# Gate operands' low parts by token halves, a first set of sigmoids one slot earlier, and one weight copy moved behind a partial sum's copy

## The chip, the cores and the metric

The kernel runs on one core of a Trainium2 chip. The metric is the device time of one execution in microseconds (us); for several runs the median is given. A core has a matrix engine (PE, with PEld for its weight loads), a vector engine (DVE), an engine for activations and copies (ACT), a third elementwise engine (POOL) and a queue that issues transfers (SP). Each engine takes its instructions strictly in the order in which the program lists them, and each waits on semaphores for the others.

## The reference

One hybrid decoder layer on 2048 tokens of 1024 channels, all in float32:

```python
xn = rms_norm(h, ln_g)
proj = jnp.einsum('bsd,de->bse', xn, w_in)          # 1024 -> 6 groups of 1024 columns
b_gate, c_gate, x_conv, g_conv, x_lru, g_lru = jnp.split(proj, splits, axis=-1)
y_conv = b_gate * causal_conv3(c_gate * x_conv);  y_conv = headnorm(y_conv) * silu(g_conv)
u = causal_conv4(x_lru) + bias
r = sigmoid(blockdiag(w_a) u + b_a);  i = sigmoid(blockdiag(w_i) u + b_i)
a = exp(8 r log_sigmoid(lam));  hidden_t = a_t hidden_{t-1} + sqrt(1 - a_t^2) i_t u_t
y_lru = headnorm(hidden) * silu(g_lru)
out = rms_norm(h + concat(y_conv, y_lru) @ w_out)
```

The two gates r and i of the recurrence come from small block-diagonal products of u. "Gate" below means these.

## The kernel before

**Products.** Channels stand on the 128 partitions, tokens along the free axis. The work is a list of 64 steps. For each half h of the sequence (1024 tokens) and each block k of 128 channels there are three steps: `l` (the columns x_lru and g_lru), `a` (c_gate and x_conv) and `b` (b_gate and g_conv); then come 16 steps `o` of the output projection. The steps of h = 0 run from about 97 to 510 us, those of h = 1 to about 1000 us. A step is a 2 x 2 block product by a Strassen-like scheme: seven products (numbered 0 to 6) of a weight operand S and an activation operand T, summed in the PSUM banks A, B and C. To keep float32 precision each operand is held as a high part, which is a rounding cast, and a low part, which is the value less the high part; a product is 12 matmuls (four inner blocks, high x high, high x low, low x high).

**Order within a step.** All instructions stand in an order written by hand; a "slot" is one product of PE. A usual step has the slots 0 to 6 with the products 0, (6 of the step before), 1, 3, 2, 4, 5. Bank A takes products 0, 1, 2 and 5, one upon the other, and three partial sums of it are copied away by ACT between them: `q1` after product 0, `u2` after product 1, `rr` after product 2 (line L1305, "the third partial sum's copy"; the tiles of u2 and rr change names every step). Product 1 can't start before q1 has been copied, product 2 not before u2, product 5 not before rr; between a sum's end and its next use lies one other product.

**Weights of the next step.** While step n runs, `s_plan` makes the seven S operands of step n+1, one piece in each slot: `add(i)` forms a sum on DVE, `hi(i)` casts a high part on ACT (L200), `lo(i)` makes a low part on DVE, or on POOL for operands 0, 4 and 6. In slot 4, beside product 2, stand `hi(3)` and `lo(1)`. The value cast by hi(3) is a difference that `add(3)` made on DVE two slots before (`raw<-raw` in the profile).

**Later work.** `at(n, f)` puts f into the n-th slot from now; `tick()` runs what is due at the start of a slot. The recurrence of block k begins when its x_lru is complete, at the end of step `l`. Its own slots count from there: 1 to 7 lie in step `a`, 8 to 14 in step `b`. `sth` (slot 5) casts the high parts of u for the gates on ACT, `stl` (slot 6) makes the low parts on DVE; two tiles `st` hold them, in st[0] the high part of channels 0 to 63 above their low part, in st[1] the low part of channels 64 to 127 above their high part. `gates(0)` in slot 8 runs four gate matmuls (st[0] twice, st[1] twice) over the first 512 tokens, `gates(1)` in slot 10 the same over the other 512; both use the same two PSUM buffers, so that `gates(1)` waits for the sigmoids that read the first. `sigs(i)` are these four sigmoids on ACT (L743, 64 x 512 each). For h = 0 `sigs(0)` stood in slot 9 and for h = 1 in slot 8; `sigs(1)` in slots 11 and 10.

Of the kernel before, what the change touches and what calls it, by code (L numbers as in the profile page):

```python
# [12 lines left out]
F32 = mybir.dt.float32  # L13
F32R = mybir.dt.float32r
AF = mybir.ActivationFunctionType
ALU = mybir.AluOpType
# [4 lines left out]
C = 512  # L21
# [17 lines left out]
def hymba_kernel(ctx: ExitStack, tc: tile.TileContext, x, xt, w_in, par, lamc, w_gate, w_out, final_g, out):  # L39
# [122 lines left out]
    def tt(out, a, b, op, eng=None):  # L162
        (eng or nc.vector).tensor_tensor(out=out, in0=a, in1=b, op=op)  # L163
# [6 lines left out]
    def low(v, hl, eng=None):  # L170
        tt(hl[1], v, hl[0].bitcast(F32), ALU.subtract, eng)

    def s_tile(dst, i):
        t = sp.tile([P, 2, C], F32R, tag="s", name="s")
        dst[i] = (t[:, 0, :], t[:, 1, :])
        return t


    def s_plan(n, r, dst):
        a11, a12, a21, a22 = r  # L180
        t, tiles = {}, {}

        def add(i):
            if i == 2:
                t[2] = aux("s1")
                tt(t[2], a21, a22, ALU.add)
            elif i == 1:
                t[1] = aux("s2")
                tt(t[1], t[2], a11, ALU.subtract)
            elif i == 3:  # L190
                tt(a21, a11, a21, ALU.subtract)
            else:
                tt(t[1], a12, t[1], ALU.subtract)

        def val(i):
            return {0: a11, 1: t.get(1), 2: t.get(2), 3: a21, 4: a12, 5: t.get(1), 6: a22}[i]

        def hi(i):
            tiles[i] = s_tile(dst, i)
            nc.scalar.copy(dst[i][0], val(i))  # L200

        def lo(i, eng=None):
            low(val(i), dst[i], eng)
            if PLAIN <= n < 3 * KT:
                at(3 if eng else 2, lambda: nc.sync.dma_start(sd[n][i], tiles[i].bitcast(F32)))

        g = nc.gpsimd if PLAIN < n < 3 * KT else None
        return [lambda: (add(2), add(1)),
                lambda: (hi(0), lo(0, g), add(3)),
                lambda: hi(1),  # L210
                lambda: (hi(3), lo(1)),
                lambda: (hi(2), lo(3), add(5)),
                lambda: (hi(4), lo(4, g), lo(2)),
                lambda: hi(5),
                lambda: (hi(6), lo(6, g), lo(5))]
# [21 lines left out]
    class TPrep:  # L237
# [8 lines left out]
        def hi(self, i, v=None):  # L246
            self.dst[i, self.j] = hl = t_tile(i, self.j)
            nc.scalar.copy(hl[0], self.val(i) if v is None else v)
# [445 lines left out]
    def lru(h, k, late=0, early=0):  # L694
        o1 = wt("o1", "xl", n=N2 + 4)
        g = wt("o2", "gl", bufs=O2)
        if h == 0:
            nc.gpsimd.memset(o1[:, 0:4], 0.0)
        else:
            nc.scalar.copy(o1[:, 0:4], hx[:, k, :])  # L700
        v = {}
        lw = [pt[:, LW + 8 * j + k:LW + 8 * j + k + 1] for j in range(4)]

        def c0():
            v["u"] = wt("u", "u")
            nc.scalar.activation(out=v["u"], in_=o1[:, 1:1 + N2], func=AF.Identity, scale=lw[0],  # L706
                                 bias=pt[:, LB + k:LB + k + 1])

        def cj(j):
            nc.vector.scalar_tensor_tensor(out=v["u"], in0=o1[:, 1 + j:1 + j + N2], scalar=lw[j],  # L710
                                           in1=v["u"], op0=ALU.mult, op1=ALU.add)

        def keep():
            if h == 0:
                nc.scalar.copy(hx[:, k, :], o1[:, N2:N2 + 4])

        def sth():
            v["st"] = st = hl_tile("st", 2)
            at(6, lambda: hl_done(2))
            for j, hi in enumerate((LO, HI)):  # L720
                nc.scalar.copy(st[j][hi], v["u"][hi])

        def stl():
            st = v["st"]
            for j, (hi, lo) in enumerate(((LO, HI), (HI, LO))):
                tt(st[j][lo], v["u"][hi], st[j][hi].bitcast(F32), ALU.subtract)

        def gates(i):
            sl = slice(i * C, (i + 1) * C)
            if i == 0:  # L730
                v["r"], v["i"] = wt("r", "r"), wt("ig", "i", bufs=IG)
            v["ps"] = ps = []
            for j in range(2):
                ps.append(pss.tile([P, C], F32, tag="s", name="gate"))
                for n in range(2):
                    nc.tensor.matmul(ps[j], v["gw"][n][:, j, :], v["st"][j][:, sl],  # L736
                                     start=(n == 0), stop=(n == 1))

        def sigs(i):
            sl = slice(i * C, (i + 1) * C)  # L740
            for j, (hi, lo) in enumerate(((LO, HI), (HI, LO))):
                for g_, src, bias in ((v["r"], hi, BA), (v["i"], lo, BI)):
                    nc.scalar.activation(out=g_[hi, sl], in_=v["ps"][j][src], func=AF.Sigmoid,  # L743
                                         bias=pt[src, bias + k:bias + k + 1])


        def s0():
            tt(v["u"], v["i"], v["u"], ALU.mult)

        def s1():  # L750
            v["T"] = wt("ig", "T", bufs=IG)
            nc.scalar.activation(out=v["T"], in_=v["r"], func=AF.Tanh, scale=nklam[:, k:k + 1])

        def s1b():
            nc.scalar.activation(out=v["r"], in_=v["r"], func=AF.Exp, scale=klam[:, k:k + 1])

        def s2():
            nc.scalar.activation(out=v["T"], in_=v["T"], func=AF.Sqrt)

        def s3():  # L760
            nc.vector.scalar_tensor_tensor(out=v["u"], in0=v["r"], scalar=1.0, in1=v["u"],
                                           op0=ALU.add, op1=ALU.mult)

        def s4():
            tt(v["u"], v["T"], v["u"], ALU.mult)

        def s5():
            r = v["r"]
            init = 0.0 if h == 0 else hl[:, k:k + 1]
            nc.vector.tensor_tensor_scan(out=r, data0=r, data1=v["u"], initial=init,  # L770
                                         op0=ALU.mult, op1=ALU.add)
            if h == 0:
                nc.vector.tensor_copy(hl[:, k:k + 1], r[:, N2 - 1:N2])

        def out_():
            finish(0, h, KT + k, v["r"], g, pt[:, LG + k:LG + k + 1])

        def gw():
            v["gw"] = load_gate_w(k)

        def put(which, bank, other):
            dst = {11: o1[:, 4:4 + C], 12: o1[:, 4 + C:4 + N2], 21: g[:, 0:C], 22: g[:, C:N2]}[which]
            combine(dst, bank, other)
            if which == 12:
                at(1, c0)
                at(2, lambda: cj(1), lambda: cj(2), keep, gw)
                at(3, lambda: cj(3))
                for slots, *fs in ((5 - early, sth), (6 - early, stl), (8, lambda: gates(0)), (9 - h - early, lambda: sigs(0)),
                                   (10, lambda: gates(1)), (11 - h - early, lambda: sigs(1)), (12, s1, s0),
                                   (13, s1b), (14, s2, s3), (15, s4), (16, s5), (17, out_)):  # L790
                    at(slots + late, *fs)
            if which == 21:
                silu(g, late, nc.vector if h and late else None)

        return put
# [236 lines left out]
    def prep(n, s):  # L1032
        if n < N:
            plan[n][s]()
# [3 lines left out]
    with tc.manual_schedule(engines={ENG.PE, ENG.Activation, ENG.DVE, ENG.Pool, ENG.SP}):  # L1038
# [177 lines left out]
        for n in range(PLAIN, N):  # L1216
            kind, h, k = steps[n]
# [28 lines left out]
            for s in range(6 if late else 8 if new or last else 7):  # L1246
# [24 lines left out]
                if new and s > 0:  # L1271
                    if s in (1, 3, 4, 5):
                        prep(n + 1, (1, 3, 4, 5).index(s) + 1)
                    elif s > 5:
                        prep(n + 2, s - 5)
                elif s > 0:
                    prep(n + 1, s - 1)
                if s == 3:
                    load_next(n + 2, 3 if late else 4)
# [17 lines left out]
                if i == 0:  # L1297
                    q1 = sm_q1[0] = sm("q1")
                    nc.scalar.copy(q1, bk["A"])  # L1299
                elif i == 1:  # L1300
                    u2 = sm_u2[0] = sm(("u2", "rr")[n % 2])
                    nc.scalar.copy(u2, bk["A"])  # L1302
                elif i == 2:
                    rr = sm(("rr", "u2")[n % 2])
                    nc.scalar.copy(rr, bk["A"])  # L1305
                    put(22, bk["B"], rr)
                    if late:
                        put(12, bk["D"], rr)
                elif i == 4:
                    put(11, bk["C"], q1)  # L1310
                elif i == 5 and not late:
                    put(12, bk["A"], None)
                elif i == 6:
                    put(21, bk["B"], u2)
# [50 lines left out]
```

## Time and profile before

| what | value |
|---|---|
| median of 3 runs | 1325.04 us (1324.93 to 1326.69) |
| the profiled execution | 1325.2 us, its span 1323.4 us |
| granted clock of the matrix engine | 0.997 |
| matmul busy | 1293.5 us of the span (98%) |
| DVE, ACT, POOL busy | 1040.3, 749.1, 245.2 us |

The profile gives for every instruction its start and duration, and for an idle time before it the event that ended it. Matmuls overlap, so a lost time on PE is read from the starts: undisturbed ones follow each other every 0.23 us.

### The profile page before, as it was taken

Reading aid. Unit: us, or ns where it says so; the run is one execution under the profiler, and the core shown is the slowest. Engines: PE = TensorE matmul, PEld = TensorE weight load, DVE = VectorE, ACT = ScalarE, POOL = GpSimd, SP = SyncE. Lnnn points to the kernel's source line nnn. Section 1 sums busy time; section 2 is a strip of 40 time slices with the busy share of each in tenths; the row PEclk is TensorE's granted clock in tenths of the full one; section 3 lists DMA queues with packets and bytes.
Section 4 is the critical chain, followed back from the end, with each engine's and each line's share of the span. In section 5 each row is a group of like instructions: output and inputs, shape, how many; then the busy total and the mean of one; then the engine's idle time right before and its main releaser. Section 6 shows DMA issues by size and latency. Waiting matters only on the chain.

```text
span 1323.4 us, 16676 instructions
## 1 busy us (share of the span) xinstructions
PE 1293.5 (98%) x5688; PEld 1058.0 (80%) x5688; DVE 1040.3 (79%) x1252; ACT 749.1 (57%) x1141; POOL 245.2 (19%) x189
## 2 busy tenths in 40 slices
PE   7989999999999999999999999999999999999997
PEld 6868878787878787878888888888888788887886
DVE  7789898999989897978566676667549777649886
ACT  7576758566675657466554545364457433445453
POOL 3204233344334340002010110101011000000000
PEclk9999999999999999999999999999999999999999
DMA  7138787888989888542789999999779887697654
GB/s 292 32 116 292 279 288 251 299 327 277 339 289 324 294 295 300 195 157 74 247 314 297 333 354 332 338 350 363 237 273 330 267 257 239 235 404 276 231 181 160
DMA packets 157958, 355.29 MB, mean 268 GB/s; under 512 B 16944, under 2 KB 51760, under 8 KB 157872
## 3 DMA queue, kind: packets, MB, share of 16 engines
q1 hardware_dynamic: 153264, 338.17, 73.7%
q0 software_dynamic: 4320, 15.73, 3.1%
q8 instruction: 45, 0.74, 0.2%
q14 instruction: 41, 0.34, 0.1%
q10 hardware_dynamic: 288, 0.32, 0.1%
HBM read 217.11 MB, written 137.04 MB: 268 GB/s over the span
## 4 chain that ended last, share of the span: by engine, by line
PE 55%; DVE 22%; DMA 10%; issue 6%; ACT 6%; SPq 1%; POOL 0%; DVEq 0%; ACTq 0%; POOLq 0%
PE bank L999 53%; DVE s L163 5%; DVE tl L163 2%; DVE u L710 2%; DMA s<-so 2%; PE gate L736 2%; DMA sd<-s 1%; DVE st L163 1%; DVE r L770 1%; DMA raw<-in_w_in_dram 1%; DMA xr<-od 1%; DVE sums L641 1%; DVE traw L163 1%; ACT i L743 1%; ACT r L743 1%
## 5 line engine op out<-in xcount | busy, mean ns | idle before, releaser
L999 PE MATMUL bank<-th,s 128*128 128x512 f32 x3632 | 1130.2, 390 | 9.6 <-ACT rr L1302 2.8
L999 PEld LDWEIGHTS bank<-th,s 128*128 128x128 f32 x3632 | 682.1, 188 | 157.4 <-ACT rr L1302 4.1
L999 PE MATMUL bank<-tl,s 128*128 128x512 f32 x1816 | 707.8, 390 | 1.8 <-DVE tl L163 1.6
L999 PEld LDWEIGHTS bank<-tl,s 128*128 128x128 f32 x1816 | 341.1, 188 | 75.0 <-DVE tl L163 3.4
L163 POOL TENSOR_TENSOR s<-raw,s 128x512 fp32r<-128x512 f32 x62 | 110.6, 1796 | 245.8 <-ACT s L200 207.4
L200 ACT CAST s<-raw 128x512 fp32r<-128x512 f32 x140 | 85.3, 618 | 76.4 <-PE bank L999 45.4
L163 POOL TENSOR_TENSOR gb<-gb,sg 128x1024 f32<-128x1024 f32 x16 | 43.4, 2712 | 336.4 <-ACT sg L669 298.2
L163 DVE TENSOR_TENSOR s<-raw,s 128x512 fp32r<-128x512 f32 (+1 forms) x125 | 93.1, 768 | 10.6 <-ACT s L1058 6.7
L163 DVE TENSOR_TENSOR s<-s,s 128x512 fp32r<-128x512 f32 x105 | 85.5, 814 | 1.9 <-ACT s L200 1.4
L163 DVE TENSOR_TENSOR tl<-traw,th 128x512 fp32r<-128x512 f32 x85 | 60.8, 748 | 23.1 <-ACT th L438 16.9
L200 ACT CAST s<-s 128x512 fp32r<-128x512 f32 x105 | 64.9, 618 | 12.6 <-DVE s L163 12.5
L710 DVE SCALAR_TENSOR_TENSOR u<-xl,pt,u 128x1024 f32<-128x1024 f32 x48 | 61.5, 1280 | 7.8 <-ACT u L706 7.2
L1299 ACT COPY q<-bank 128x512 f32<-128x512 f32 x58 | 34.0, 585 | 54.0 <-PE bank L999 44.4
L820 DVE SCALAR_TENSOR_TENSOR t<-p,pt,t 128x1024 f32<-128x1024 f32 x32 | 46.5, 1454 | 16.6 <-ACT t L817 15.9
L743 ACT ACTIVATE r<-gate,pt 64x512 f32<-64x512 f32 x64 | 43.8, 684 | 17.4 <-PE gate L736 16.6
L1302 ACT COPY rr<-bank 128x512 f32<-128x512 f32 x31 | 18.1, 584 | 55.2 <-PE bank L999 55.2
L163 DVE TENSOR_TENSOR st<-u,st 64x1024 fp32r<-64x1024 f32 x32 | 47.2, 1476 | 1.0
L1302 ACT COPY u<-bank 128x512 f32<-128x512 f32 x27 | 15.8, 585 | 53.4 <-PE bank L999 53.4
L163 DVE TENSOR_TENSOR raw<-raw 128x512 f32<-128x512 f32 x41 | 44.9, 1095 | 0.2
L438 ACT CAST th<-traw 128x512 fp32r<-128x512 f32 x64 | 36.2, 618 | 15.6 <-DVE traw L163 13.9
L743 ACT ACTIVATE i<-gate,pt 64x512 f32<-64x512 f32 x64 | 43.8, 685 | 1.1
L163 DVE TENSOR_TENSOR traw<-traw 128x512 f32<-128x512 f32 x60 | 42.3, 709 | 2.2 <-DMA traw<-in_w_out_dram 1.1
(169 smaller groups left out, 1267.4 us busy)
## 6 DMA issues: line engine op xcount, KB each, us to landing
sd<-s SPq DMA_DIRECT2D x151, 512.0 KB
s<-sd SPq DMA_DIRECT2D x151, 512.0 KB
raw<-in_w_in_dram SPq DMA_DIRECT2D x104, 256.0 KB
raw<-yd SPq DMA_DIRECT2D x64, 256.0 KB
traw<-in_w_out_dram SPq DMA_DIRECT2D x64, 256.0 KB
so<-so SPq DMA_DIRECT2D x22, 512.0 KB
s<-so SPq DMA_DIRECT2D x22, 512.0 KB
yd<-gl SPq DMA_DIRECT2D x32, 256.0 KB
```

Source lines behind the costliest of these rows:

```text
L163: (eng or nc.vector).tensor_tensor(out=out, in0=a, in1=b, op=op)
L200: nc.scalar.copy(dst[i][0], val(i))
L438: nc.scalar.copy(self.dst[i, j][0], self.r[i, j])
L641: nc.vector.tensor_reduce(out=sums[0][:, kt * R:(kt + 1) * R].rearrange("p (q b) -> p q b", q=4), in_=y.rearrange("p (b q a) -> p q b a", ...
L710: nc.vector.scalar_tensor_tensor(out=v["u"], in0=o1[:, 1 + j:1 + j + N2], scalar=lw[j], in1=v["u"], op0=ALU.mult, op1=ALU.add)
L736: nc.tensor.matmul(ps[j], v["gw"][n][:, j, :], v["st"][j][:, sl], start=(n == 0), stop=(n == 1))
L743: nc.scalar.activation(out=g_[hi, sl], in_=v["ps"][j][src], func=AF.Sigmoid, bias=pt[src, bias + k:bias + k + 1])
L770: nc.vector.tensor_tensor_scan(out=r, data0=r, data1=v["u"], initial=init, op0=ALU.mult, op1=ALU.add)
L820: nc.vector.scalar_tensor_tensor(out=tcur["t"], in0=p[:, 2 + j:2 + j + N2], scalar=cw[j], in1=tcur["t"], op0=ALU.mult, op1=ALU.add)
L999: nc.tensor.matmul(bank, a[:, js], b, start=start and n == 0, stop=stop and n == 2, skip_group_check=more)
L1299: nc.scalar.copy(q1, bk["A"])
L1302: nc.scalar.copy(u2, bk["A"])
```

## The change

It has three parts.

1. `stl` makes the low parts in four pieces of 64 x 512 instead of two of 64 x 1024, first both tiles' first token half, then both tiles' second half. This holds for all 16 recurrences.
2. `sigs(0)` is always due in slot 8, in the same slot as `gates(0)`. That moves it for the blocks 1 to 7 of h = 0; for the others it was there already.
3. In slots whose product is number 2, hi(3) of the next step's weights is held back and issued right behind the copy `rr`. In the whole program 32 of the 58 copies change places with it.

```diff
+    held = [None]
+    def defer(f):
+        if held[0] is None:
+            f()
+        else:
+            held[0].append(f)
+    def release():
+        fs, held[0] = held[0] or (), None
+        for f in fs:
+            f()
...
-                lambda: (hi(3), lo(1)),
+                lambda: (defer(lambda: hi(3)), lo(1)),
...
         def stl():
             st = v["st"]
-            for j, (hi, lo) in enumerate(((LO, HI), (HI, LO))):
-                tt(st[j][lo], v["u"][hi], st[j][hi].bitcast(F32), ALU.subtract)
+            for i in range(2):
+                sl = slice(i * C, (i + 1) * C)
+                for j, (hi, lo) in enumerate(((LO, HI), (HI, LO))):
+                    tt(st[j][lo, sl], v["u"][hi, sl], st[j][hi, sl].bitcast(F32), ALU.subtract)
...
-    (8, lambda: gates(0)), (9 - h - early, lambda: sigs(0)),
+    (8, lambda: gates(0)), (8, lambda: sigs(0)),
...
                 elif s > 0:
+                    held[0] = [] if i == 2 else None
                     prep(n + 1, s - 1)
...
                     nc.scalar.copy(rr, bk["A"])
+                    release()
                     put(22, bk["B"], rr)
```

No instruction is added or removed on PE, ACT, POOL or SP, and on PE, POOL and SP the order is the same; DVE has 32 instructions more. Line numbers of the changed kernel are 13 to 16 higher.

On ACT, in step `l` of block 4 of h = 0 (slots 3 to 5), before: a sigmoid of the step before, a weight cast, a square, then hi(3) as the cast of a `raw` tile, and the copy `rr` behind it.

```order
L669 ACTIVATE sg_2667<-gb_2406 128x1024
L200 CAST s_2669<-s2_2627 128x512
L661 ACTIVATE r_2410<-r_2410 128x1024
L200 CAST s_2697<-raw_2506 128x512
L1305 COPY rr_2712<-bank_2603 128x512
L200 CAST s_2719<-s1_2625 128x512
```

The same place now:

```order
L682 ACTIVATE sg_2675<-gb_2414 128x1024
L213 CAST s_2677<-s2_2635 128x512
L674 ACTIVATE r_2418<-r_2418 128x1024
L1321 COPY rr_2718<-bank_2611 128x512
L213 CAST s_2720<-raw_2514 128x512
L213 CAST s_2727<-s1_2633 128x512
```

The copy and the cast have changed places; what is behind them stands as before.

On ACT, where step `a` of block 4 ends and its step `b` begins (the gates of block 4), before: the copy of p out of bank A, hi(5) as the cast of an `s2` tile, the copy q1, and the four sigmoids of the first token half.

```order
L200 CAST s_2907<-raw_2673 128x512
L799 COPY p_2756<-bank_2763 128x512
L200 CAST s_2938<-s2_2788 128x512
L1299 COPY q1_2953<-bank_2940 128x512
L743 ACTIVATE r_2928<-gate_2930,pt_164 64x512
L743 ACTIVATE i_2929<-gate_2930,pt_164 64x512
L743 ACTIVATE r_2928<-gate_2933,pt_164 64x512
L743 ACTIVATE i_2929<-gate_2933,pt_164 64x512
L817 ACTIVATE t_2989<-p_2756,pt_164 128x1024
```

The same place now:

```order
L213 CAST s_2917<-raw_2681 128x512
L814 COPY p_2764<-bank_2771 128x512
L758 ACTIVATE r_2938<-gate_2940,pt_164 64x512
L758 ACTIVATE i_2939<-gate_2940,pt_164 64x512
L758 ACTIVATE r_2938<-gate_2943,pt_164 64x512
L758 ACTIVATE i_2939<-gate_2943,pt_164 64x512
L213 CAST s_2952<-s2_2796 128x512
L1315 COPY q1_2967<-bank_2954 128x512
L832 ACTIVATE t_2999<-p_2764,pt_164 128x1024
```

The four sigmoids have moved ahead of hi(5) and q1.

On DVE, ahead of the gates of block 4, before: the sum xx, the two low parts `st`, then low parts and sums for the next step's weights.

```order
L163 TENSOR_TENSOR xx_2881<-bank_2844,u2_2879 128x512
L163 TENSOR_TENSOR st_2857<-u_2759,st_2857 64x1024
L163 TENSOR_TENSOR st_2858<-u_2759,st_2858 64x1024
L163 TENSOR_TENSOR s_2864<-raw_2672,s_2864 128x512
L163 TENSOR_TENSOR s2_2788<-raw_2673,s2_2788 128x512
```

The same place now:

```order
L163 TENSOR_TENSOR xx_2889<-bank_2852,u2_2885 128x512
L163 TENSOR_TENSOR st_2865<-u_2767,st_2865 64x512
L163 TENSOR_TENSOR st_2866<-u_2767,st_2866 64x512
L163 TENSOR_TENSOR st_2865<-u_2767,st_2865 64x512
L163 TENSOR_TENSOR st_2866<-u_2767,st_2866 64x512
L163 TENSOR_TENSOR s_2887<-raw_2680,s_2887 128x512
L163 TENSOR_TENSOR s2_2796<-raw_2681,s2_2796 128x512
```

Two instructions have become four, and a gate matmul over the first 512 tokens waits for the first two of them alone.

More of the change, by code (lines that the diff above doesn't have):

```diff
@@ L787, in put @@
                 at(3, lambda: cj(3))
-                for slots, *fs in ((5 - early, sth), (6 - early, stl), (8, lambda: gates(0)), (9 - h - early, lambda: sigs(0)),
+                for slots, *fs in ((5 - early, sth), (6 - early, stl), (8, lambda: gates(0)), (8, lambda: sigs(0)),
                                    (10, lambda: gates(1)), (11 - h - early, lambda: sigs(1)), (12, s1, s0),
```

## The prediction

> **What bounds the kernel now.** I read the page first, then who waited for whom on PE by stretches of the span, then the timelines around each wait.
>
> ```profile
> span 1323.4 us, 16676 instructions
> PE 1293.5 (98%) x5688; PEld 1058.0 (80%) x5688; DVE 1040.3 (79%) x1252; ACT 749.1 (57%) x1141; POOL 245.2 (19%) x189
> ```
>
> PE is the bound, so the change can only gain what PE stands idle. PE's waits from 100 to 505 us (first four rows), then from 40 to 100 (the next two), then the two largest of 505 to the end (us in total, times, longest):
>
> ```profile
> PE gate L736 <- DVE st L163: 1.4, 6, 0.2
> PE gate L736 <- ACT i L743: 1.2, 7, 0.2
> PE bank L999 <- ACT rr L1305: 1.0, 1, 1.0
> PE bank L999 <- ACT u L1305: 0.7, 1, 0.7
> ...
> PE gate L736 <- ACT i L743: 2.5, 2, 2.0
> PE gate L736 <- DVE st L163: 1.1, 2, 0.6
> ...
> PE bank L999 <- ACT rr L1302: 2.8, 3, 1.3
> PE bank L999 <- DVE xx L163: 1.9, 1, 1.9
> ```
>
> In the middle stretch all waits are of the three kinds that the change touches: low parts of the gates, sigmoids, third copies. The view's idle understates them. Starts around the gates of block 4 (start, duration, idle before in brackets):
>
> ```profile
> 314.86 0.39 PE L736 MATMUL gate<-st,bl 128*128 128x512 f32 x1
> 315.47 0.47 PE L736 MATMUL gate<-st,bh 128*128 128x512 f32 x1 [0.23 <-DVE st L163]
> ...
> 316.01 0.39 PE L999 MATMUL bank<-th,s 128*128 128x512 f32 x1
> ...
> 321.70 0.39 PE L736 MATMUL gate<-st,bl 128*128 128x512 f32 x1
> 322.26 0.50 PE L736 MATMUL gate<-st,bh 128*128 128x512 f32 x1 [0.18 <-ACT i L743]
> ...
> 322.83 0.39 PE L999 MATMUL bank<-th,s 128*128 128x512 f32 x1
> ```
>
> Three matmuls take 3 x 0.23 us when nothing is late. Here they took 1.15 and 1.13: each wait costs 0.45 to 0.47 us, its idle plus some 0.25.
>
> **Third copies (part 3).** In step `l` of block 4:
>
> ```profile
> 288.06 2.87 POOL L163 TENSOR_TENSOR gb<-gb,sg 128x1024 f32<-128x1024 f32 x1 [3.05 <-ACT sg L669]
> 288.60 2.88 DVE L163 TENSOR_TENSOR raw<-raw 128x512 f32<-128x512 f32 x1
> ...
> 288.40 1.06 ACT L661 ACTIVATE r<-r 128x1024 f32<-128x1024 f32 x1
> 291.56 0.62 ACT L200 CAST s<-raw 128x512 fp32r<-128x512 f32 x1 [2.11 <-issue]
> 292.09 0.58 ACT L1305 COPY rr<-bank 128x512 f32<-128x512 f32 x1
> ...
> 292.26 0.96 PE L999 MATMUL bank<-th,s 128*128 128x512 f32 x2
> 293.06 0.39 PE L999 MATMUL bank<-tl,s 128*128 128x512 f32 x1
> ...
> 473.21 0.97 PE L999 MATMUL bank<-th,s 128*128 128x512 f32 x2
> ```
>
> add(3) on DVE takes 2.88 us beside POOL's product, hi(3) waits for it from 289.46 to 291.56, and the copy rr stands behind hi(3) although its sum was complete by about 290 (product 5 was due at 292.5, and product 4, 12 x 0.23 us, lies between). PE's second matmul in the row at 292.26 belongs to product 5 and waits: 0.80 us for two matmuls, 0.35 lost. This recurs in blocks 4 to 7 (the last at 473.21): 4 x 0.35 = 1.4. In blocks 2 and 3 it is the 1.0 and 0.7 of the first fence, with 0.25 each 2.2. Sum 3.6. With the copy first it ends near 290.6, 1.9 us ahead of need. What moves back is hi(3): it still waits for add(3), so it starts at 291.56 as now, and the casts behind it come no later. In steps `a` and `b` hi(3) used to run in the copy's wait and now runs 0.5 us later; its reader lo(3) stands on DVE behind the sum that needs rr itself, so nothing waits. Taken: 3.6 (bounds 2.8, if block 2, whose ACT work is longer, keeps part, and 3.6).
>
> **Sigmoids (part 2).** ACT around the same gates:
>
> ```profile
> 314.88 0.59 ACT L799 COPY p<-bank 128x512 f32<-128x512 f32 x1 [2.12 <-PE bank L999]
> 316.68 0.62 ACT L200 CAST s<-s 128x512 fp32r<-128x512 f32 x1 [1.21 <-DVE s L163]
> 318.94 0.59 ACT L1299 COPY q<-bank 128x512 f32<-128x512 f32 x1 [1.64 <-PE bank L999]
> 319.42 0.69 ACT L743 ACTIVATE r<-gate,pt 64x512 f32<-64x512 f32 x1
> ...
> 321.53 0.68 ACT L743 ACTIVATE i<-gate,pt 64x512 f32<-64x512 f32 x1
> ```
>
> ACT idled before 316.68 and again before 318.94, and only then did the four sigmoids (0.70 us apart). Now they follow the p copy and the gate matmuls: 315.5 to 318.3. Behind them wait hi(5) (to 318.9) and the copy q1 (to 319.5, as late as now or 0.4 later). q1 is needed by the product behind `gates(1)`, at 322.4 without stalls, so the delay is covered by one whole product and the four gate matmuls, 2.9 us; lo(5) stands on DVE beyond 322, also covered. `gates(1)`, ready at about 321, finds its buffers free since 318.3. Seven waits of 0.45: 3.1. ACT's table loads stay the same in number and place.
>
> **Low parts (part 1).**
>
> ```profile
> 311.87 3.45 DVE L163 TENSOR_TENSOR st<-u,st 64x1024 fp32r<-64x1024 f32 x2
> 312.84 1.40 POOL L163 TENSOR_TENSOR s<-raw,s 128x512 fp32r<-128x512 f32 x1 [2.15 <-ACT s L200]
> ...
> 558.00 2.47 DVE L163 TENSOR_TENSOR st<-u,st 64x1024 fp32r<-64x1024 f32 x2
> ...
> 503.84 1.29 DVE L163 TENSOR_TENSOR tl<-traw,th 128x512 fp32r<-128x512 f32 x2 [4.43 <-ACT th L438]
> ```
>
> The pair took 2.47 us alone at 558, and 3.45 with POOL's low part beside its second half. A 64 x 512 piece isn't in the trace; nearest is a 128 x 512 of the same kind, 0.69 long and, in a row of its kind, started every 0.60. So four pieces take from 2.5 (4 x 0.60 + 0.09) to 2.84 us (each starting 0.03 behind the end of the last, 4 x 0.71, as the pair at 558 does: 1.25 apart at 1.22 each). I take 2.84, since the pieces alternate between the partition halves as the pair does: 0.35 more per recurrence. (At 2.5 us the terms for the first and last blocks below would be 0.35 better each, and the sum 10.9.) [...]
>
> The first two pieces are done 1.42 us after the start instead of 2.5 or 3.45: at 313.3, or 314.6 if POOL gets in between. The gate matmuls ask for them at 314.63 and 315.09, less up to 0.4 that parts 2 and 3 bring PE ahead of DVE. So the wait goes in blocks 4 to 7, and in block 1, where an unlisted wait of 0.35 stands. In blocks 2 and 3 PE gains 1.2 us more on DVE and I count half. Of 0.35 + 6 x 0.47 = 3.1 remain 2.6 (bounds 0 and 3.1).
>
> **DVE as the next bound.** Its idle rows in the cycle of three steps from 315.47, and the cycle itself (length, then busy time of PE, PEld, DVE, ACT, POOL):
>
> ```profile
> 321.67 0.69 DVE L163 TENSOR_TENSOR xx<-bank,rr 128x512 f32<-128x512 f32 x1 [1.89 <-PE bank L999]
> ...
> 329.13 1.48 DVE L163 TENSOR_TENSOR u<-i,u 128x1024 f32<-128x1024 f32 x1 [0.76 <-ACT i L743]
> ...
> 331.92 0.69 DVE L163 TENSOR_TENSOR gb<-bank,rr 128x512 f32<-128x512 f32 x1 [0.70 <-ACT rr L1305]
> ...
> 315.47:375.77 60.30, 59.81 (x260) 48.57 (x261) 56.55 (x58) 38.67 (x56) 23.64 (x15) 1.00 0.87 304
> ```
>
> From 331.92 to the end of the next `st` DVE doesn't idle. PE's cycle shrinks by 0.35 + 0.45 + 0.47 to 59.0. DVE's, from one wait for PE (xx) to the next, is 60.3 - 1.9 = 58.4, plus 0.35 for the pieces, less 0.5 because rr (and so gb) comes sooner: 58.3. It stays the shorter by 0.7.
>
> **First and last blocks.**
>
> ```profile
> 73.94 0.62 ACT L1145 CAST th<-traw 128x512 fp32r<-128x512 f32 x1 [0.31 <-DVE traw L163]
> ...
> 76.37 0.50 PE L736 MATMUL gate<-st,bh 128*128 128x512 f32 x1 [2.01 <-ACT i L743]
> ...
> 509.81 0.50 PE L999 MATMUL bank<-th,s 128*128 128x512 f32 x1 [0.40 <-ACT rr L1302]
> ```
>
> Block 0: PE gets its gates 1.3 us sooner, but the next wait (2.0) ends with sigmoids behind casts that wait for DVE; DVE is 0.35 later, so PE loses 0.3 there. After block 7 DVE idled 4.43 us for casts (the row at 503.84) that stood behind the moved sigmoids; the casts come some 2.8 us sooner, the wait at 509.81 goes (0.65), and the one for xx (1.9), at the end of a busy stretch of DVE, shrinks if that lead lasts, less 0.35 for the pieces. Bounds 0.3 and 3; taken 1.2, the nearer to the visible 0.65, since DVE waits for transfers and casts on the way.
>
> **Sum.** 3.6 + 3.1 + 2.6 + 1.2 - 0.3 = 10.2. The profiled execution took 1325.2, 0.2 above the median; the prediction is 1315.0.
>
> **Rivals.**
> - *DVE takes over in blocks 2 to 7.* For: 0.7 us of margin in 59. Against: three idle rows remain. One more full wait behind POOL per cycle (the pair's 3.45 against 2.47 shows 1.0) puts it 0.3 beyond PE, 6 x 0.3 = 1.8, and `st` is late again, 2.6: gain 5.8, time 1319.4. [...]
> - *Only the waits move.* If the stretch of DVE up to the wait for xx at about 565 is fixed by transfers and not by PE, PE's lead is spent there: within 0.2% (2.65 us, about what a measurement of this kernel can tell from no change), 1323.5. Against: the stretch begins with DVE waiting for ACT and PE.
> - *Slower: q1 behind the sigmoids.* ACT is in order; if the sigmoids end over 2.9 us later than worked out, PE stands before its second product in seven steps. At 2 us beyond, 14 us are lost against 10.2 gained: 1329. It decides from 1.5 us beyond. For h = 1, where the sigmoids stand in this slot already, the waits from 505 on show no such wait.
>
> **Numbers.** The sum: 0.65, own range 1312 to 1317.5. DVE: 0.23, 1317.5 to 1321. Moved: 0.08. Slower: 0.04. Range 1311.5 to 1320.5: below, the upper bounds together (3.6 + 3.1 + 3.1 + 3 = 12.8) and a little; above, most of the second case. Faster 0.9, same 0.06, slower 0.04.
>
> **What would show it.** Right: from 100 to 505 us no PE wait for L1305's copy (L1321 now), for `i` or `st`; rr 1.9 us sooner in `l`; four `st` pieces 0.7 apart; xx waits some 1 us per cycle. Wrong: a PE wait for q1 or for low parts `s`, or a longer one at 565.

## The result and the profile after

The changed kernel took 1315.14 us (median of 5 runs, 1314.92 to 1316.99) against 1326.42 of the kernel before, run beside it (5 runs, 1324.93 to 1327.33): ratio 0.9921, 95% interval 0.9910 to 0.9933. The forecast was 1315.0. The profiled execution took 1314.92, its span 1313.1. One execution of a kernel shown further below took 1854.53 us at a granted clock of 0.655 and is left out of every median and ratio.

The profile's page, then the view of who waited for whom on PE, for 100 to 500 us, for 40 to 100, and the two largest rows from 500 to the end (us in total, times, longest):

```profile
span 1313.1 us, 16711 instructions
PE 1289.5 (98%) x5688; PEld 1061.0 (81%) x5688; DVE 1046.0 (80%) x1284; ACT 748.7 (57%) x1141; POOL 250.0 (19%) x189
...
PE bank L1014 <- ACT q L1315: 0.7, 1, 0.7
...
PE gate L751 <- ACT i L758: 3.6, 2, 3.4
...
PE bank L1014 <- ACT rr L1318: 1.6, 2, 1.3
PE bank L1014 <- DVE xx L163: 1.3, 1, 1.3
```

In the middle stretch the three kinds of wait that the change touches are gone. The one row left there, for q1, stood just ahead of 100 us before. In the first block the total stayed (2.5 + 1.1 then, 3.6 now), but it is now one long wait.

The waits' idle understates what PE loses (0.18 us idle for 0.45 lost at 503.22, below), so I also added up, over the whole trace, by how much each matmul starts later than 0.2267 us after the one before it. These sums come from all rows of PE's timeline; starts before 13 us and delays under 0.02 us are left out. Each sum is that of one execution. Of the prediction's seven waits for sigmoids one, at 503.22 us, lies behind the middle stretch, so its 0.45 stands in the row behind:

| lost on PE, us | before | after | gained | term in the prediction |
|---|---|---|---|---|
| 13 to 40 us | 4.14 | 4.14 | 0 | 0 |
| 40 to 97 (block 0) | 5.93 | 7.63 | -1.70 | -0.3 |
| 97 to 105 | 1.00 | 1.00 | 0 | 0 |
| 105 to 500 | 9.53 | 0.19 | 9.34 | 3.6 + 2.65 + 2.6 = 8.85 |
| 500 to 577 | 5.49 | 3.54 | 1.95 | 0.45 + 1.2 = 1.65 |
| 577 to the end | 4.60 | 3.73 | 0.87 | 0 |
| sum | 30.69 | 20.23 | 10.46 | 10.2 |

The spans differ by 10.3. The wait at 503.22 in the kernel before:

```profile
503.22 0.50 PE L736 MATMUL gate<-st,bh 128*128 128x512 f32 x1 [0.18 <-ACT i L743]
```

The gates and step `l` of block 4, from the timelines of PE, ACT, DVE and POOL (start, duration, idle before it in brackets):

```profile
311.53 0.39 PE L751 MATMUL gate<-st,bh 128*128 128x512 f32 x1
311.76 0.39 PE L751 MATMUL gate<-st,bl 128*128 128x512 f32 x1
311.98 0.39 PE L751 MATMUL gate<-st,bh 128*128 128x512 f32 x1
...
287.24 0.59 ACT L1321 COPY rr<-bank 128x512 f32<-128x512 f32 x1 [0.54 <-PE bank L1014]
288.82 0.62 ACT L213 CAST s<-raw 128x512 fp32r<-128x512 f32 x1 [0.99 <-DVE raw L163]
...
312.27 0.68 ACT L758 ACTIVATE r<-gate,pt 64x512 f32<-64x512 f32 x1
...
315.07 0.62 ACT L213 CAST s<-s 128x512 fp32r<-128x512 f32 x1
315.60 0.58 ACT L1315 COPY q<-bank 128x512 f32<-128x512 f32 x1
...
308.80 3.83 DVE L163 TENSOR_TENSOR st<-u,st 64x512 fp32r<-64x512 f32 x4
309.75 1.62 POOL L163 TENSOR_TENSOR s<-raw,s 128x512 fp32r<-128x512 f32 x1 [2.12 <-ACT s L213]
...
318.12 0.69 DVE L163 TENSOR_TENSOR xx<-bank,rr 128x512 f32<-128x512 f32 x1 [1.04 <-PE bank L1014]
...
311.53:370.56 59.03, 59.03 (x262) 48.80 (x261) 57.05 (x60) 38.92 (x56) 24.64 (x15) 1.00 0.89 314
```

The gate matmuls follow each other every 0.23 us. ACT's copy `rr` waits for PE instead of standing behind the cast, which still waits for DVE's `raw`. The sigmoids begin beside the gates, and the copy q1 starts 4.07 us behind the first gate matmul (315.60 less 311.53). It stood 4.3 behind before (318.94 less the 314.63 of the prediction), so it came no later. The last row is one cycle of three steps, from one block's gates to the next's: 59.03 us, forecast 59.0. DVE's wait for PE at xx, its margin, is 1.04 us.

### The profile page after: what moved, and what is told of

The parts are those of the page before. It is cut to its first block, busy times and chain, and to the rows that moved or that the text cites. A ratio compares the mean times of both kernels' runs of the same rounds, so it can differ in the third digit from the quotient of the medians.

```text
span 1313.1 us, 16711 instructions
## 1 busy us (share of the span) xinstructions
PE 1289.5 (98%) x5688; PEld 1061.0 (81%) x5688; DVE 1046.0 (80%) x1284; ACT 748.7 (57%) x1141; POOL 250.0 (19%) x189
## 4 chain that ended last, share of the span: by engine, by line
PE 82%; DVE 8%; DMA 5%; ACT 3%; issue 2%; SPq 0%; POOL 0%; ACTq 0%; DVEq 0%
PE bank L1014 79%; DMA s<-so 2%; DVE tl L163 2%; PE gate L751 2%; DVE traw L163 1%; DMA tl<-td 1%; DMA zr<-rsd 1%; DMA xr<-od 1%; DMA fg<-in_final_g_dram 1%; DVE u L723 1%; ACT i L758 0%; DVE s L163 0%; ACT r L758 0%; ACT th L451 0%; PE tp L554 0%
## 5 line engine op out<-in xcount | busy, mean ns | idle before, releaser
L163 POOL TENSOR_TENSOR s<-raw,s 128x512 fp32r<-128x512 f32 x62 | 115.1, 1870 | 231.1 <-ACT s L213 176.0
L163 DVE TENSOR_TENSOR st<-u,st 64x512 fp32r<-64x512 f32 x64 | 53.8, 841 | 2.0
L1318 ACT COPY u<-bank 128x512 f32<-128x512 f32 x27 | 15.8, 585 | 52.4 <-PE bank L1014 52.4
L1321 ACT COPY u<-bank 128x512 f32<-128x512 f32 x31 | 18.1, 585 | 43.6 <-PE bank L1014 43.5
```

## The experiments

All were timed in five rounds beside the kernel before. Its median was 1325.47 us in the first group (the three parts alone, the whole pieces in block 0), 1325.98 in the second (gates two products later, tile by tile, the added pieces), and 1325.77 in the third (gates one product later, no sigmoids).

**Part 1 alone.** The kernel before, with only this:

```diff
-            for j, (hi, lo) in enumerate(((LO, HI), (HI, LO))):
-                tt(st[j][lo], v["u"][hi], st[j][hi].bitcast(F32), ALU.subtract)
+            for i in range(2):
+                sl = slice(i * C, (i + 1) * C)
+                for j, (hi, lo) in enumerate(((LO, HI), (HI, LO))):
+                    tt(st[j][lo, sl], v["u"][hi, sl], st[j][hi, sl].bitcast(F32), ALU.subtract)
```

> Part 1 alone (the low parts of the gates in four pieces) in the kernel before. Theory A, the three parts' gains add and block 0 pays for the pieces with a half-rate spell of PE: from 100 to 500 us the waits for st go (3.1 us), the waits for the sigmoids and for the third copy stay or grow a little, block 0 loses 1.7, so 1.0 to 1.5 us faster than before, span near 1322. Theory B, the loss in block 0 comes from elsewhere: 2.7 to 3.1 us faster. Theory C, a wait taken away only moves to the next gate: within 0.5 us of before.

Measured: 1324.0 us, ratio 0.9986 (0.9977 to 0.9994), which is theory A. The middle stretch lost 6.26 instead of 9.53, and no wait for `st` is left in it. But block 0 lost 8.04 instead of 5.93, and 500 to 577 us 0.36 more. So this part wins 3.3 in the middle and gives 2.1 of it back in block 0 and 0.4 behind.

**Part 2 alone.**

```diff
-    (9 - h - early, lambda: sigs(0)),
+    (8, lambda: sigs(0)),
```

> Part 2 alone (sigmoids of the first token half one slot earlier in blocks 1 to 7 of h = 0). Theory A: seven waits of 0.45 go (3.1), and after block 7 the casts that stood behind the sigmoids come sooner (1.5 to 2 us more between 500 and 577): 4.5 to 5 us faster than before; no change in block 0. Theory B, the gain after block 7 needs the other parts: 3.1. Theory C, q1 behind the sigmoids makes PE wait: slower, and a PE wait for q1 in the trace.

Measured: 1320.77 us, ratio 0.9966 (0.9954 to 0.9977). The middle lost 6.88 (2.65 less). From 500 to 577 us it lost 3.26 instead of 5.49, 2.2 less. One wait for sigmoids (0.45) is part of that; the other 1.8 is what the sum had as "after block 7", and the sigmoids alone bring it. That is theory A of the three.

**Part 3 alone.**

```diff
-                lambda: (hi(3), lo(1)),
+                lambda: (defer(lambda: hi(3)), lo(1)),
...
+                    held[0] = [] if i == 2 else None
...
                     nc.scalar.copy(rr, bk["A"])
+                    release()
```

> Part 3 alone (the weight cast hi(3) behind the third copy). Theory A: the waits for the third copy go in blocks 2 to 7, 3.6 us faster than before; block 0 and the stretch after 505 as before. Theory B, PE's lead on DVE makes the low parts of the gates later: part of it comes back as longer st waits, 1.5 to 2.5 us faster.

Measured: 1323.48 us, ratio 0.9983 (0.9974 to 0.9991), which is theory B. PE's waits from 105 to 500 us, and one gate matmul each of blocks 1 and 2:

```profile
PE gate L749 <- DVE st L163: 3.6, 7, 1.0
PE gate L749 <- ACT i L756: 1.1, 6, 0.2
...
132.49 0.47 PE L749 MATMUL gate<-st,bh 128*128 128x512 f32 x1 [0.78 <-DVE st L163]
...
193.17 0.47 PE L749 MATMUL gate<-st,bh 128*128 128x512 f32 x1 [1.00 <-DVE st L163]
```

Before, the wait for `st` had 1.4 in all and 0.2 at most. The third copies' waits are gone (3.65 us by the starts), but the middle gained only 1.6, because PE now came earlier to low parts that DVE still finished at its own time. In blocks 2 and 3 the waits for `st` grew from 0.47 and 0.48 us of starts to 1.24 and 0.97: the wait moved. In block 1 it grew from 0.35 to 1.02 for another reason, since no third copy was late ahead of it: in this execution block 0 lost 1.1 us less (4.81 against 5.93), as its matmuls ran at full rate behind the wait of 2.0 us (see block 0 below). With block 0 alike the gain would have been some 0.7 higher, by estimate.

**Parts 1 and 3 without part 2.** The changed kernel with the sigmoids' old slot.

> The changed kernel with the first sigmoids back in their old slot: parts 1 and 3 of the change without part 2. Theory A (part 3 alone handed most of its 3.45 us to the waits for low parts, and part 1 takes these waits away, so that together they are worth more than the sum): lost time from 105 to 500 us about 2.5 us (seven waits for i of 0.33), the xx wait at 565 back near 2.2: 1319.5 to 1320.5. Theory B (parts 1 and 3 simply add as they did alone, 1.5 and 2.0): about 1322.

Measured: 1319.75 us, ratio 0.9957 (0.9944 to 0.9969), as theory A has it. PE's only wait from 105 to 500 us:

```profile
PE gate L751 <- ACT i L758: 1.2, 7, 0.2
```

The middle lost 3.27. All but 0.2 of it is the seven waits for sigmoids, the last of which now comes ahead of 500 us. Low parts and third copies lost 6.8 there before, so parts 1 and 3 won 6.6 together, where alone they won 3.27 + 1.6 = 4.9. Of the 1.7 between, some 0.7 is the block 1 of part 3's execution. The rest fits this: part 3 brings PE forward, and part 1 has the operand ready for it. In the ratios the two make 0.0014 and 0.0017 alone and 0.0043 together, which points the same way, but each interval reaches about 0.001 to either side, so the times don't settle it.

**Is DVE next?** Low parts of the second half were made again, in blocks 1 to 7 of h = 0, once (as shown) or three times.

```diff
+            if h == 0 and not early:
+                for _ in range(1):
+                    tt(st[1][LO, C:N2], v["u"][HI, C:N2], st[1][HI, C:N2].bitcast(F32), ALU.subtract)
```

> The changed kernel with one piece of the second token half made twice in blocks 1 to 7 of h = 0: 0.71 us more for DVE per cycle of three steps. Theory A, DVE has about 1.0 us of idle time per cycle (its wait for PE at xx): no change beyond 0.5 us, and that wait shrinks to about 0.3. Theory B, DVE is already as much the bound as PE: 0.7 x 6 = 4 us slower.

> The same with the piece made four times instead of once: 2.1 us more for DVE per cycle. Theory A, margin 1.0 (and 0.5 in the two waits for ACT): 0.6 to 1.1 us per cycle beyond it, 4 to 7 us slower than the changed kernel, with st waits back. Theory B, DVE the bound: 2.1 x 6 = 12.8 us slower. Theory C, the waits of DVE are not margin at all (PE much ahead everywhere): no change.

Measured: 1315.25 us (0.9922, 0.9909 to 0.9936) and 1320.33 (0.9957, 0.9944 to 0.9971), theory A in both. DVE's wait for xx from 200 to 490 us, in the changed kernel and with one more piece:

```profile
DVE xx L163 <- PE bank L1014: 4.0, 5, 1.0
```

```profile
DVE xx L163 <- PE bank L1017: 0.9, 3, 0.4
```

One piece of 0.7 us a cycle went into this wait (4.0 to 0.9 over five cycles) and cost nothing. With three the wait is gone, and PE lost 3.91 from 105 to 500 us and 5.09 from 500 to 577, 3.7 and 1.5 more than the changed kernel, or some 0.75 a cycle. Three pieces take 2.1 us a cycle, so DVE had some 1.3 to give, by estimate: 0.8 to 1 in the wait for xx, the rest in other waits.

**The order of the pieces.** Both halves of one tile, then the other tile.

```diff
-            for i in range(2):
-                sl = slice(i * C, (i + 1) * C)
-                for j, (hi, lo) in enumerate(((LO, HI), (HI, LO))):
+            for j, (hi, lo) in enumerate(((LO, HI), (HI, LO))):
+                for i in range(2):
+                    sl = slice(i * C, (i + 1) * C)
```

> The changed kernel with the four pieces in another order: both token halves of the first tile, then both of the second. Theory A, a piece starts behind the end of the last only when it changes partition halves: the two pieces of one tile start 0.60 us apart, the four take 2.6 instead of 2.84. Theory B, all pieces start 0.71 apart whatever the halves: 2.84. For the time: the second gate matmul of the first half waits for the third piece, which is done 2.0 (A) or 2.1 us after the start, and with POOL's low part in between 3.2, while it is asked for about 3.2 to 3.4 us after the start: 0 to 2 us slower than the changed kernel.

Measured: 1315.56 us, ratio 0.9923 (0.9911 to 0.9935). DVE's four pieces ahead of the first recurrence of h = 1, in the changed kernel, then tile by tile, and there a gate of block 2:

```profile
548.18 2.82 DVE L163 TENSOR_TENSOR st<-u,st 64x512 fp32r<-64x512 f32 x4
```

```profile
548.06 2.61 DVE L163 TENSOR_TENSOR st<-u,st 64x512 fp32r<-64x512 f32 x4
...
548.06 1.29 DVE L163 TENSOR_TENSOR st<-u,st 64x512 fp32r<-64x512 f32 x2
...
192.90 0.47 PE L751 MATMUL gate<-st,bh 128*128 128x512 f32 x1 [0.65 <-DVE st L163]
```

Two pieces on the same partitions take 1.29 us, 0.60 apart; where the partitions change it is 0.71 (2.61 = 0.60 + 0.71 + 0.60 + the last one's 0.69). That saves 0.2 us. But the second tile's first half, which the second pair of gate matmuls reads, comes third instead of second, and PE lost 0.81 and 0.51 us in blocks 2 and 3. In the time the two can't be told apart.

**Block 0.** First, its low parts left whole:

```diff
-            for i in range(2):
-                sl = slice(i * C, (i + 1) * C)
+            for sl in ((slice(0, N2),) if early else (slice(0, C), slice(C, N2))):
```

> The changed kernel with the low parts of block 0 in two pieces as before, all others in four. Theory A, the half-rate spell of PE at 77 to 84 us follows from the longer idle time (3.4 us) that the pieces make there: the spell ends by 80.5 as before the change and the kernel is 1.7 us faster than the changed one. Theory B, only DVE's delay of 0.35 counts: 0.3 to 0.4 faster.

Measured: 1314.76 us (4 runs), ratio 0.9916 (0.9903 to 0.9928). In the profiled execution block 0 lost 4.82 instead of 7.63, and the span is 2.7 shorter. But this execution was the fastest of the four (1312.24 us, the others 1314.58 to 1315.58), and the median is 0.4 below the changed kernel's, with overlapping intervals. So the profile shows the loss, and the times don't settle its size. In the profiled executions with the changed kernel's pieces and gates in block 0 it lost 7.2 to 8.0 us (five kernels), and in those with whole low parts 4.8 to 6.0 (four kernels). Its gates for the second half, then those of the changed kernel and of the kernel before. Below the rows of the first two stands the stretch from 77 to 84 us (busy time of PE, PEld, DVE, ACT and POOL, granted clock, DMA share, GB/s):

```profile
76.55 0.50 PE L750 MATMUL gate<-st,bh 128*128 128x512 f32 x1 [2.00 <-ACT i L757]
...
78.52 0.39 PE L1013 MATMUL bank<-th,s 128*128 128x512 f32 x1
78.75 0.40 PE L1013 MATMUL bank<-tl,s 128*128 128x512 f32 x1
78.98 0.62 PE L1013 MATMUL bank<-th,s 128*128 128x512 f32 x2
...
77.00:84.00 7.00, 6.33 (x29) 5.02 (x28) 4.91 (x7) 6.78 (x12) 0.10 (x1) 1.00 0.01 2
```

```profile
77.05 0.79 PE L751 MATMUL gate<-st,bh 128*128 128x512 f32 x1 [3.41 <-ACT i L758]
...
79.47 0.63 PE L1014 MATMUL bank<-th,s 128*128 128x512 f32 x1
79.90 0.63 PE L1014 MATMUL bank<-tl,s 128*128 128x512 f32 x1
...
82.88 1.04 PE L1014 MATMUL bank<-th,s 128*128 128x512 f32 x2
83.74 0.41 PE L1014 MATMUL bank<-tl,s 128*128 128x512 f32 x1
...
77.00:84.00 7.00, 6.77 (x16) 4.84 (x17) 4.92 (x6) 6.75 (x11) 0.10 (x1) 0.52 0.01 2
```

```profile
78.79 0.63 PE L999 MATMUL bank<-th,s 128*128 128x512 f32 x1
79.22 0.63 PE L999 MATMUL bank<-tl,s 128*128 128x512 f32 x1
79.64 0.88 PE L999 MATMUL bank<-th,s 128*128 128x512 f32 x2
80.36 0.39 PE L999 MATMUL bank<-tl,s 128*128 128x512 f32 x1
```

After the wait of 3.41 us the matmuls start 0.43 us apart, half the rate, until 83.74; before, until 80.36; with whole low parts not at all. The granted clock of the stretch says the same: 0.52 with the pieces and 1.00 with whole low parts.

Then the second half's gates and sigmoids two products later, so that the first half's sigmoids are done:

```diff
-    (10, lambda: gates(1)), (11 - h - early, lambda: sigs(1)),
+    (10 + 2 * early, lambda: gates(1)), (11 - h + early, lambda: sigs(1)),
```

> The changed kernel with the second half's gate matmuls of block 0 two slots later and their sigmoids with them, so that PE has two more part products to do while ACT comes to the first sigmoids. Theory A, PE's idle time at 73 to 77 us and the half-rate spell behind it go (7 us of lost starts), of which ACT's own chain (casts up to 95.8 us, then the copy q1) gives back some: 3.5 to 5 us faster than the changed kernel, and the wait for q1 near 100 us is longer than 0.7. Theory B, PE runs ahead only to stand at the next low part of block 0's weights: under 1 us faster. Theory C: the recurrence of block 0 comes two slots later and delays block 1: slower.

Measured: 1315.58 us, ratio 0.9927 (0.9914 to 0.9939): no gain, where 3.5 to 5 us were expected. PE at the end of block 0, and ACT there:

```profile
95.46 0.39 PE L1014 MATMUL bank<-th,s 128*128 128x512 f32 x1
101.84 0.79 PE L1014 MATMUL bank<-th,s 128*128 128x512 f32 x1 [5.98 <-ACT q L1315]
102.43 0.63 PE L1014 MATMUL bank<-tl,s 128*128 128x512 f32 x1
...
85.28 0.63 ACT L213 CAST s<-s 128x512 fp32r<-128x512 f32 x1 [2.92 <-DVE s L163]
...
100.68 0.62 ACT L213 CAST s<-s 128x512 fp32r<-128x512 f32 x1
101.20 0.58 ACT L1315 COPY q<-bank 128x512 f32<-128x512 f32 x1
```

The wait at the gates went, and all of it came back at q1. Two products later the sigmoids stand behind a cast that waits 2.92 us for DVE (the row at 85.28). They start at 85.80 instead of 80.04 (1.7 of that is a later start of the whole block in this execution: its first late gate matmul is at 68.50 instead of 66.79) and push everything behind them on ACT, which then shows no idle time up to q1.

Two kernels put the gates one product later. In the first, one weight cast moves behind the sigmoids as well, so that ACT's order stays that of the changed kernel; in the second the cast stands ahead of them, and the part of the diff behind the dots is missing.

```diff
-    (10, lambda: gates(1)), (11 - h - early, lambda: sigs(1)),
+    (10 + early, lambda: gates(1)), (11 - h, lambda: sigs(1)),
...
+            if s == 3:
+                prep(3, 1)
-            if s in (1, 2, 3, 4, 6, 7):
+            if s in (1, 3, 4, 6, 7):
```

> The changed kernel with the second token half's gates of block 0 one product later on PE; ACT and DVE keep their order. Theory A (PE's clock and its idle time at these gates set block 0): the gates meet sigmoids that are nearly done, PE idles about 0.6 and 0.7 us there instead of 3.4 and 0.2, no matmuls 0.43 us apart follow, and the loss in this place goes from 7.2 to about 1.8 us. ACT had 2.27 + 1.67 us in hand before q1 at 100.83, so that the wait for q1 grows by about 1.5 us. Net 3.5 to 4.5 us: about 1311. Theory B (the end of block 0 is set by ACT's row from 80 to 100 us, whatever PE does): the wait only moves to q1 at 100, 1314 to 1316.

> The same, but with one weight cast, which waits for DVE until about 82.8 us, ahead of the second sigmoids on ACT. On PE the same order as with the gates one product later. Theory A (ACT's in-order row up to q1 is the next bound, with about 3.9 us in hand): the sigmoids come 3 us later, ACT's slack is used up, PE waits 4 to 5 us for q1 near 100: 1313.5 to 1315.5, 2 to 4 us slower than the kernel without the cast in front. Theory B (DVE or transfers bound that stretch, ACT's row is not tight): the two kernels agree within 1 us.

Measured: 1312.46 us (0.9897, 0.9877 to 0.9917) and 1312.9 (0.9899, 0.9881 to 0.9918). The first lies between its two theories, and there is no comparable trace of it to say how ACT's room was spent. Of the second, the gates and the next wait on PE, and the cast and the sigmoids on ACT:

```profile
76.85 0.50 PE L751 MATMUL gate<-st,bh 128*128 128x512 f32 x1 [0.69 <-ACT i L758]
...
78.25 0.50 PE L751 MATMUL gate<-st,bh 128*128 128x512 f32 x1 [0.67 <-ACT i L758]
...
97.12 0.50 PE L1014 MATMUL bank<-th,s 128*128 128x512 f32 x1 [1.79 <-ACT q L1315]
...
79.84 0.62 ACT L213 CAST s<-raw 128x512 fp32r<-128x512 f32 x1
80.36 0.69 ACT L758 ACTIVATE r<-gate,pt 64x512 f32<-64x512 f32 x1
```

PE idles 0.69 and 0.67 us as expected, at full rate, and the wait for q1 grew from 0.73 to 1.79. Block 0 and the 8 us behind it lost 6.1 instead of 8.6. My difference between the two kernels was wrong: I had read the cast as waiting for DVE until 82.8, but it reads a piece that was there already and runs at 79.84 without a wait, so the sigmoids came about 0.5 us later and not 3. That the two agree within 1 us therefore says nothing about ACT's room, which this pair was meant to test. Both are below the changed kernel by 2.2 to 2.7 us in the medians, 0.0022 to 0.0024 in the ratios. Their intervals overlap the changed kernel's slightly, so a better version is likely, but its size isn't settled.

## Why the prediction was right, point by point

- *PE is the bound; only idle time can be won.* Held: lost time fell by 10.46, the span by 10.3.
- *Third copies 3.6, sigmoids 3.1, low parts 2.6.* By the starts the kernel before lost 3.65 at third copies, 3.17 at low parts and 2.7 at six waits for sigmoids from 105 to 500 us, and 0.45 at the seventh behind. All of it went but 0.19 at low parts. So copies and sigmoids came out as forecast and the low parts gave 3.0. The reason given for counting half of blocks 2 and 3 (PE gains on DVE there) is what part 3 alone shows, but with pieces the waits go almost entirely: the halving was too careful. The split isn't a property of the parts. Alone they won 2.65 (sigmoids), 3.27 (low parts) and 1.6 (third copies); the third copies are worth their 3.65 only where the low parts don't take the wait over.
- *Pieces 0.71 apart, 2.84 in all.* Measured 2.82 with nothing beside them (3 x 0.71 + 0.69), and 0.60 apart within one tile (tile by tile). The upper value was right.
- *DVE stays the shorter by 0.7.* Held: the cycle is 59.03, and 0.7 more a cycle is free while 2.1 isn't. With POOL's low part beside them the pieces took 3.83 (308.80) against 2.82, so the 1.0 us that this rival counts on is there, but the first two pieces were in time.
- *q1 no later than 0.4.* Held, see block 4.
- *Block 0, -0.3.* This step failed in size: -1.70. PE's idle time there is unchanged, 0.61 + 0.46 + 2.01 + 0.50 before and 3.41 + 0.18 after. The pieces bring the first gates forward, the second ones wait for the same sigmoids, so the idle time collects in one place. What I left out is the half rate seen behind this wait: in the profile after, a spell of 6.7 us with matmuls 0.43 us apart follows 3.4 us idle (five of five profiled executions with a wait of 3.4 to 3.5 us there have a spell of this kind); after 2.0 us idle two of four have none and two have 2.6 and some 3.3 us.
- *After block 7, 1.2.* Somewhat too small: 1.5 up to 577 us without the seventh wait for sigmoids, 1.8 with the sigmoids alone, inside the bounds of 0.3 and 3. The wait at 509.81 went, and the wait for DVE before 565 fell from 1.89 to 1.32, as the casts came sooner:

```profile
493.81 1.29 DVE L163 TENSOR_TENSOR tl<-traw,th 128x512 fp32r<-128x512 f32 x2 [0.96 <-ACT th L451]
...
555.48 0.50 PE L1014 MATMUL bank<-th,s 128*128 128x512 f32 x1 [1.32 <-DVE xx L163]
```

- *Nothing behind 577 us.* 0.87 came there, 0.74 of it at one wait for u2 near 1030, behind casts that wait for a transfer. It can't be put down to the change. That wait cost 1.35 us of starts before and 0.60 after, but among the other kernels with all three parts it is between 0.4 (three more pieces) and 1.5 (gates two products later), with 1.35 tile by tile and 1.40 with one more piece. So it varies from trace to trace, and why is open.

The errors of -1.4 in block 0, +0.5 in the middle, +0.3 after block 7 and +0.87 behind nearly cancel. That the sum came out so close is luck; that the waits of the middle stretch would go, and why, was right.

## What to carry to other kernels

Add up lost time from the starts, stretch by stretch, not from the waits' idle, and do it for each part alone: a removed wait can be taken over by the next operand in line, as in blocks 2 and 3 here, and two edits can then be worth more than their sum. Do it with more than one trace where you can, since one wait, near 1030 us, differed by up to 1 us between traces of kernels that all have the change. Before moving a wait on the matrix engine, ask whether idle time is removed or only gathered: in block 0 one wait of 3.4 us and one of 0.2 cost more than four of the same sum (7.63 us lost against 5.93). And before delaying an engine's work, read how much room its in-order row has up to the next instruction that somebody waits for, and which waits it will then stand behind: in block 0 one product later probably won some 2 us, two won nothing.

## What the runs showed of the hardware

The half rate was seen behind the waits of 3.4 to 3.5 us (five of five) and 5.98 us, in two of four executions behind 2.0 us, behind waits of 2.25 us (parts 1 and 3 without part 2) and 2.29 (three more pieces), and behind the 1.79 above, where these two stand 1.4 us later:

```profile
98.55 0.63 PE L1014 MATMUL bank<-tl,s 128*128 128x512 f32 x1
98.98 0.63 PE L1014 MATMUL bank<-th,s 128*128 128x512 f32 x1
```

These two start 0.43 us apart. It was also seen near 16 us, with the same short waits of at most 0.9 us, in four of twelve profiled executions (with one more piece the matmuls from 18.25 to 19.96 us start 0.43 us apart) and not in the others. That is 1.2 to 1.5 us from one execution to the next, and so probably part of why the counted runs of one kernel differ by 1 to 8 us and their granted clock lies between 0.994 and 0.999. What sets these spells is open: after 2.0 us idle two of four executions have none, and after 1.79 us there is one.
